# A decoder layer on one core: inverse at seven steps, first projections by operands as loaded, another order at the seam into the up projection

## The chip, the core and the metric

The kernel runs on one core of one Trainium2 chip. The core has TensorE (PE, the matrix engine; PEld is its loading of weights), VectorE (DVE), ScalarE (ACT), GpSimd (POOL) and SyncE (SP), which issues most of the DMAs. Every engine works through its own instructions in order and waits for others by semaphores. The metric is the device time of one execution in microseconds; less is better.

## The reference, cut

One layer of a hybrid decoder: 1024 tokens of width 1024, everything in float32.

```python
h = rms_norm(x, norm1_g);  proj = h @ w_in
p_rwkv, p_sb, q_mem, gate_logits = split(proj)
y_a = rwkv7_branch(p_rwkv, ...)             # 8 heads x 64: token shift, decay, delta-rule state over time
y_b = stick_breaking_branch(p_sb, ...)      # 8 heads x 64: causal, weights by cumulative log(1 - sigmoid)
y_m = memory_branch(q_mem, mem, ...)        # 4 heads x 128: softmax over 256 memory tokens
merged = sum_b sigmoid(gate_b) * (y_b @ w_branch[b])
x = x + merged @ w_out
h2 = rms_norm(x, norm2_g) @ w_up            # 1024 -> 5632
a = causal depthwise convolution of width 3 over h2, plus bias
x = x + (silu(a_gate) * a_val) @ w_down     # 2816 -> 1024
```

## The kernel before

**Arithmetic.** A product of float32 matrices is made of three matmuls on PE: each operand is split into a rounded part `hi` (a copy to fp32r, mostly on ACT) and a rest `lo` (operand minus `hi`, on POOL for weights, on DVE for activations), and hi x hi, hi x lo and lo x hi are added up in PSUM. A matmul takes a 128x128 block of one operand as weights and 512 columns of the other. Weight tiles are `wr` (as loaded), `wh` (L80) and `wl` (L81); `xhi` and `xlo` (L185, L186) are the split input.

**The order of the work.** Python writes the program; a scheduler in the tile framework then places each engine's instructions by priorities. Instructions that are `pinned` or kept in program order keep the order in which Python writes them; generators that `yield` are woven step by step (`weave`), so that a main chain of work and a stream of filler take turns.

1. `startup` (0 to 47 us): the parameters, three tiles of `w_in` (12, 13 and 4; 128x1024 each) and the eight row blocks of x are loaded by SP, one behind the other: weight, x, x, weight, and so on. All are split whole, ACT squares each block (L197), DVE adds the squares up as they come (L199), and for k in 0..7 PE multiplies block k with all three weights. The row norm goes in between at k = 4 and 6.
2. `rwkv_prep` (to some 300 us), woven with the filler `pump`: the rest of the projections, gates and the branches' first parts.
3. `sb_attn`, stick-breaking attention (300 to some 680 us), woven with `pump`. Its scans (L848) run on DVE; PE transposes what ACT makes of them (L860). Beside it the **inverse** of small triangular blocks runs on DVE: `inverse` has 62 steps of a product (L474, `it<-inst`) and a sum (L476, `inst<-inst,it`), and then 16 DMAs from the POOL queue (L483, `td<-inst`). `pumped` advances it by `pace[0]` / 10 of an instruction for each item of the filler; `pace[0]` is 6 from stick-breaking attention on. What is left is drained when the branches begin.
4. `mem_attn`, memory attention (680 to 775 us), in units of a head and half the tokens, woven with `pump`. A unit has a *front* (PE: `g<-A,qk`; DVE: maximum `mxt`, L1058, and its scaled negative `nb`, L1061; ACT: four exponentials, L1064; DVE: reciprocal and normalisation, L1068 and L1070), a *middle* (PE transposes; ACT copies them from `g` to `at`, L1079) and a *back* (PE: `mm<-at,A`; ACT copies the result, L1089). Round v has the front of unit v, the back of v-4 and the middle of v-2. The queries' own split is L1026 to L1028 (`qk`). The filler between them is a projection *gate*: ACT copies it out of PSUM (L749), DVE scales it by the row norm (L750, `w<-w,nrt`), ACT takes the sigmoid (L753). ACT loads another table between exponentials and the sigmoid.
5. `stage2` (the recurrence over time), group norm, branches, `out_proj` (775 to 1183 us). `out_proj` makes 128 tokens at a time (tt = 0..7): PE, then the residual sum and the squares (L1252 to L1254), the norm's power on POOL (L172, `ss<-rs,half`), and transposes into `raw0`, `raw1`.
6. **The seam** (1177 to 1222 us) and `up_phase` (to 1610 us). The up projection is a Strassen-Winograd product: per pair of weight columns 7 half-size products (numbers 1 to 7; 40 and 41 are the two parts of 4) in place of 8. Its operands on the token side are the blocks themselves ("11", "21", "22") and sums of them (T1 to T4), split by ACT and DVE or POOL (`hi`, `lo`; L1291, L1296). On the weight side POOL makes sums (L1402, L1403, L1414, L1415) and rests (L1386). `prep1`, `prep2` and `prep3` prepare a pair's weights; `step(n, i)` does product i of pair n and the sums on DVE (`u`: L1500, L1507, L1508, L1517, L1524; the memset of its first two columns L1438); `conv` is the convolution (L1446 to L1452). At the seam the last 128 tokens (columns 384 to 512 of the operands, `new`) are late, so pairs 0 and 1 run in an order of their own.
7. `down_phase` (1610 to 1824 us): 7 products x 11 steps. Each step splits an activation block `da` (L1654, L1656) and a weight block `dw` (L1655, L1657, or with a sum L1649) three steps ahead. `complete` adds a finished quarter of the output to the residual on DVE (L1676), `release` sends it out.

Of the kernel before, what the change touches and what calls it, by code (L numbers as in the profile page):

```python
# [19 lines left out]
D = 1024  # L20
C = 64
# [28 lines left out]
class Trunk:  # L50
# [70 lines left out]
    def setup(self):  # L121
# [11 lines left out]
        nc.sync.dma_start(self.params, self.I["params"])  # L133
# [34 lines left out]
    def rsqrt(self, out, ss, n, scale, eps):  # L168
        nc = self.nc
        t = self.small("rs", [128, 16])  # L170
        nc.vector.tensor_scalar(t[:, :n], ss, scale, eps, ALU.mult, ALU.add)
        nc.gpsimd.tensor_tensor(out, t[:, :n], self.half[:, :n], ALU.pow)  # L172

    def startup(self):
        nc = self.nc
        self.xhi, self.xlo, sqs, ws = [], [], [], []
        first = (12, 13, 4)
        for k in range(8):
            if k < 6 and k % 2 == 0:
                raww = self.load_w(self.I["w_in"][first[k // 2]])  # L180
            raw = self.t4("at")
            nc.sync.dma_start(raw, self.I["xT"][k * 128 : (k + 1) * 128, :])
            hi = self.pool_x.tile([128, 1024], F32R, name=f"xhi{k}")
            lo = self.pool_x.tile([128, 1024], F32R, name=f"xlo{k}")
            nc.scalar.activation(hi, raw, AF.Copy, scale=self.par("g1", k))  # L185
            nc.vector.scalar_tensor_tensor(lo, raw, self.par("g1", k), hi.bitcast(F32), ALU.mult, ALU.subtract)  # L186
            self.xhi.append(hi)
            self.xlo.append(lo)
            if k < 6 and k % 2 == 0:
                if k < 4:  # L190
                    hi = self.pool_wt.tile([128, 1024], F32R, name=self.nm("wh"), tag="wh", bufs=2)
                    lo = self.pool_wt.tile([128, 1024], F32R, name=self.nm("wl"), tag="wl", bufs=2)
                else:
                    hi, lo = self.t4(dt=F32R), self.t4(dt=F32R)
                ws.append(self.split_raw(raww, hi, lo))
            sq = self.t4("qk")
            nc.scalar.activation(sq, raw, AF.Square)  # L197
            if k:
                nc.vector.tensor_tensor(sq, sq, sqs[-1], ALU.add)  # L199
            sqs.append(sq)  # L200
        nc.sync.dma_start(self.kon, self.I["kon"])
        self.lora = self.t4("A")
# [3 lines left out]
        self.xin = lambda k: [[t[k][:, h * 512 : (h + 1) * 512] for h in range(2)] for t in (self.xhi, self.xlo)]  # L206
        pps = [[self.ps(t), self.ps(t)] for t in ("mm", "mm", "g")]
        for k in range(8):
            ks = slice(k * 128, (k + 1) * 128)
            for w, pp in zip(ws, pps):  # L210
                self.mm3(pp, [a[:, ks] for a in w], self.xin(k), k == 0, k == 7)
            if k == 4:
                self.row_norm(sqs[-1])
            elif k == 6:
                self.row_spread()
# [1001 lines left out]
    def out_proj(self):  # L1217
# [21 lines left out]
        def norm(tt, pp):  # L1239
            x = self.t4() if tt < 7 else l4("x7", F32)  # L1240
            sq = self.t4() if tt < 7 else self.pool_l.tile([128, 1024], F32, name="sq7", tag="sp", bufs=1)
            nc.sync.dma_start(x, self.I["x"][tt * 128 : (tt + 1) * 128, :])
            st = self.small("ss2", [128, 3])
# [8 lines left out]
            self.rsqrt(rs, rs, 1, 1.0 / D, 1e-6)  # L1252
# [54 lines left out]
        def late(tt):  # L1307
# [3 lines left out]
            elif tt == 5:  # L1311
                sums(0, 256)
            elif tt == 6:
                sums(256, 384)
# [13 lines left out]
        def weight_sums(w1):  # L1328
            w2, s = l4("wsec", F32), l4("wsum", F32)
            nc.sync.dma_start(w2, self.I["w_up"][1])  # L1330
            nc.gpsimd.tensor_tensor(s[:, :512], w2[:, :512], w2[:, 512:], ALU.add)
            nc.gpsimd.tensor_tensor(s[:, 512:], s[:, :512], w1[:, :512], ALU.subtract)
            self.early.append(self.split_raw(s, l4("wsh", F32R), l4("wsl", F32R)))
            nc.gpsimd.tensor_tensor(w2[:, :512], w1[:, :512], w2[:, :512], ALU.subtract)
            nc.gpsimd.tensor_tensor(s[:, 512:], w1[:, 512:], s[:, 512:], ALU.subtract)
# [7 lines left out]
        for tt in range(2, 8):  # L1343
            pp = mm((tt,), {3: (0,), 6: (1,)} if tt == 2 else {4: (tt - 1,)})[0]
            if tt == 5:
                weight_sums(w1)
# [571 lines left out]
```

## Time and profile before

| | |
|---|---|
| median of 3 runs | 1827.49 us (1827.4 to 1828.59) |
| profiled execution | 1825.74 us |
| its span | 1824.0 us |
| granted PE clock, mean | 0.995 |
| PE busy | 1785.2 us, 98% |
| DVE, ACT, POOL busy | 65%, 47%, 43% |
| first and last matmul | 7.79 and 1819.98 us |
| 90 matmuls of 512 columns at full speed | 20 us |

A row of the timeline gives start and length in us, engine, line, operation, `out<-in` by the names of the program, shapes, and in brackets how long the engine had been idle and what ended it. The waits list what PE waited for: total us, times, longest. PEclk is the granted share of the full TensorE clock.

### The profile page before, as it was taken

Reading aid. Unit: us, or ns where it says so; the run is one execution under the profiler, and the core shown is the slowest. Engines: PE = TensorE matmul, PEld = TensorE weight load, DVE = VectorE, ACT = ScalarE, POOL = GpSimd, SP = SyncE. Lnnn points to the kernel's source line nnn. Section 1 sums busy time; section 2 is a strip of 40 time slices with the busy share of each in tenths; the row PEclk is TensorE's granted clock in tenths of the full one; section 3 lists DMA queues with packets and bytes.
Section 4 is the critical chain, followed back from the end, with each engine's and each line's share of the span. In section 5 each row is a group of like instructions: output and inputs, shape, how many; then the busy total and the mean of one; then the engine's idle time right before and its main releaser. Section 6 shows DMA issues by size and latency. Waiting matters only on the chain.

```text
span 1824.0 us, 27302 instructions
## 1 busy us (share of the span) xinstructions
PE 1785.2 (98%) x10468; PEld 1444.6 (79%) x10468; DVE 1182.7 (65%) x1622; ACT 866.2 (47%) x1553; POOL 789.8 (43%) x447
## 2 busy tenths in 40 slices
PE   8999999999999999899999999989999999999999
PEld 6777778888787887677777878868888888888877
DVE  5667674787888854234542892487776777794595
ACT  5544344556566635434544333554544445444343
POOL 2323353322231433212323541587767777545454
PEclk9999999999999999899999999999999999999999
DMA  4255564211112323468754562322322323395475
GB/s 183 70 163 183 181 218 157 73 41 44 53 56 87 115 92 94 128 236 288 252 181 156 180 233 98 121 86 89 120 98 87 121 93 121 112 347 194 138 259 179
DMA packets 122341, 261.29 MB, mean 143 GB/s; under 512 B 28506, under 2 KB 43098, under 8 KB 122083
## 3 DMA queue, kind: packets, MB, share of 16 engines
q1 hardware_dynamic: 84738, 193.71, 32.3%
q10 hardware_dynamic: 33696, 53.23, 8.0%
q0 software_dynamic: 3776, 12.62, 2.3%
q8 instruction: 82, 1.34, 0.3%
q14 instruction: 49, 0.39, 0.1%
HBM read 178.99 MB, written 80.48 MB: 142 GB/s over the span
## 4 chain that ended last, share of the span: by engine, by line
PE 71%; DVE 3%; issue 3%; ACT 2%; POOL 2%; DMA 2%; SPq 0%; ACTq 0%; POOLq 0%; DVEq 0%
PE mm L115 58%; PE g L115 10%; PE g L105 3%; POOL dw L1657 1%; DVE at L1208 1%; DMA A<-yd 1%; DVE mg L1215 0%; DVE at L1207 0%; DVE w L750 0%; DVE inst L476 0%; DMA u<-in_w_down_dram 0%; DMA mrd<-w 0%; DMA x<-in_x_dram 0%; ACT w L753 0%; DMA wr<-in_w_out_dram 0%
## 5 line engine op out<-in xcount | busy, mean ns | idle before, releaser
L81 POOL TENSOR_TENSOR wl<-wr,wh 128x1024 fp32r<-128x1024 f32 x77 | 198.9, 2584 | 504.0 <-ACT wh L80 504.0
L115 PE MATMUL mm<-xhi,wh 128*128 128x512 f32 x784 | 262.2, 415 | 8.7 <-ACT xhi L185 7.8
L115 PE MATMUL mm<-xlo,wh 128*128 128x512 f32 x784 | 245.1, 394 | 0.9 <-DVE xlo L186 0.9
L115 PE MATMUL mm<-xhi,wl 128*128 128x512 f32 x784 | 243.1, 392 | 0.0
L115 PEld LDWEIGHTS mm<-xlo,wh 128*128 128x128 f32 x784 | 148.1, 189 | 34.7 <-DVE xlo L186 1.6
L115 PEld LDWEIGHTS mm<-xhi,wl 128*128 128x128 f32 x784 | 147.9, 189 | 33.3 <-POOL wl L81 0.5
L115 PEld LDWEIGHTS mm<-xhi,wh 128*128 128x128 f32 x784 | 137.8, 191 | 36.6 <-ACT xhi L185 7.8
L80 ACT ACTIVATE wh<-wr 128x1024 fp32r<-128x1024 f32 x77 | 81.6, 1060 | 145.7 <-PE mm L115 95.9
L115 PE MATMUL mm<-dw,da 128*128 128x512 f32 x528 | 121.2, 390 | 0.4 <-DVE da L1656 0.3
L115 PE MATMUL mm<-BT,l 128*128 128x512 f32 x504 | 117.9, 389 | 1.6 <-POOL l L1386 1.6
L1657 POOL TENSOR_TENSOR dw<-draw,dw 128x512 fp32r<-128x512 f32 x55 | 80.9, 1478 | 83.4 <-ACT dw L1655 83.4
L115 PEld LDWEIGHTS mm<-dw,da 128*128 128x128 f32 x528 | 98.9, 188 | 22.2 <-DVE da L1656 1.1
L848 DVE TENSOR_TENSOR_SCAN at<-at,nrt 128x128 f32<-128x128 f32 (+3 forms) x64 | 88.1, 1386 | 40.3 <-ACT at L842 40.2
L115 PEld LDWEIGHTS mm<-BT,l 128*128 128x128 f32 x504 | 94.5, 188 | 21.6 <-POOL l L1386 2.0
L115 PE MATMUL mm<-BT,wh 128*128 128x512 f32 x352 | 108.8, 390 | 1.6 <-DVE BT L1296 0.9
L115 PE MATMUL mm<-B,wh 128*128 128x512 f32 x352 | 108.5, 389 | 0.0
L1656 DVE TENSOR_TENSOR da<-draw,da 128x512 fp32r<-128x512 f32 x77 | 64.8, 851 | 59.6 <-ACT da L1654 57.1
L115 PE MATMUL g<-dw,da 128*128 128x512 f32 x396 | 92.5, 395 | 2.1 <-POOL dw L1657 1.1
L1386 POOL TENSOR_TENSOR l<-it,l 128x1024 fp32r<-128x1024 f32 x21 | 50.8, 2419 | 92.1 <-ACT l L1383 92.1
L115 PEld LDWEIGHTS g<-dw,da 128*128 128x128 f32 x396 | 75.4, 191 | 18.6 <-POOL dw L1657 1.4
L750 DVE TENSOR_TENSOR w<-w,nrt 128x1024 f32<-128x1024 f32 x24 | 48.8, 2033 | 63.6 <-ACT w L749 52.7
L1654 ACT ACTIVATE da<-draw 128x512 fp32r<-128x512 f32 x77 | 48.3, 629 | 81.5 <-PE mm L115 38.9
(332 smaller groups left out, 3987.1 us busy)
## 6 DMA issues: line engine op xcount, KB each, us to landing
wr<-in_w_in_dram SPq DMA_DIRECT2D x50, 512.0 KB, 3.6
draw<-actd SPq DMA_DIRECT2D x77, 256.0 KB, 3.4
draw<-in_w_down_dram SPq DMA_DIRECT2D x55, 256.0 KB, 4.6
at<-scr SPq DMA_DIRECT2D x24, 512.0 KB, 6.0
wr<-in_w_up_dram SPq DMA_DIRECT2D x22, 512.0 KB, 3.5
actd<-gall ACTq DMA_DIRECT2D x44, 256.0 KB, 3.2
rw<-in_w_up_dram SPq DMA_DIRECT2D x20, 512.0 KB, 3.6
gsd<-w ACTq DMA_DIRECT2D x18, 512.0 KB, 2.8
```

The lines of the kernel that those rows point to most:

```text
L80: self.nc.scalar.activation(hi, raw, AF.Copy)
L81: self.nc.gpsimd.tensor_tensor(lo, raw, hi.bitcast(F32), ALU.subtract)
L105: self.pinned(self.nc.tensor.transpose(out, in_, self.ident[:n, :n]))
L115: self.pinned(self.nc.tensor.matmul(*a, **k))
L750: nc.vector.tensor_tensor(g, g, self.nrb, ALU.mult)
L848: self.pinned(nc.vector.tensor_tensor_scan(sn[:, :W][:, ::-1], sn[:, :W][:, ::-1], self.nrt[:, 1152 - W :][:, ::-1], 1.0, ALU.mult, ALU.max))
L1208: nc.vector.tensor_tensor(g[:, hs], g[:, hs], o[:, hs], ALU.add)
L1386: nc.gpsimd.tensor_tensor(lo, src, hi.bitcast(F32), ALU.subtract)
L1654: self.pinned(nc.scalar.activation(A[:, 0], a, AF.Copy))
L1656: self.pinned(nc.vector.tensor_tensor(A[:, 1], a, A[:, 0].bitcast(F32), ALU.subtract))
L1657: nc.gpsimd.tensor_tensor(Wt[:, 1], w, Wt[:, 0].bitcast(F32), ALU.subtract)
```

## The change

The diff has four parts.

**Start.** The first weight tile comes in two parts of 256 and 768 columns; eight columns of the parameters come over the ACT queue first, the rest later. Eleven matmuls on a zeroed tile are put ahead of everything on PE. The first two blocks of x are split in halves, the products are written in the order in which their operands arrive, and the squares, their sums and the row norm come later.

```diff
-        nc.sync.dma_start(self.params, self.I["params"])
...
+        nc.scalar.dma_start(self.params[:, 0:8], self.I["params"][:, 0:8])
+        idle = self.t4("ys", BF16, 512)
+        nc.vector.memset(idle, 0.0)
+        pt = self.ps("g")
+        for _ in range(11):
+            nc.tensor.matmul(pt, idle[:, :128], idle, start=True, stop=True)
...
+            for hs in halves if k < 2 else [slice(0, 1024)]:
+                nc.scalar.activation(hi[:, hs], raws[k][:, hs], AF.Copy, scale=self.par("g1", k))
...
+        units(0, [0])
+        raw1 = self.load_w(self.I["w_in"][13])
+        load_x()
+        split_x()
+        ws.append(self.split_raw(raw1, *pair()))
+        units(0, [1])
...
+        units(1, [4])
+        self.row_norm(sqs[-1])
+        units(1, [5, 6, 7])
+        units(2, [4])
+        self.row_spread()
+        units(2, [5, 6, 7])
```

SP's queue at the start of the program, before (`wr`: weight tiles; `at`: blocks of x):

```order
L133 DMA params<-in_params_dram 128x246
L76 DMA wr_99<-in_w_in_dram 128x1024
L182 DMA at_101<-in_xT_dram 128x1024
L182 DMA at_113<-in_xT_dram 128x1024
L76 DMA wr_122<-in_w_in_dram 128x1024
L182 DMA at_124<-in_xT_dram 128x1024
L182 DMA at_137<-in_xT_dram 128x1024
L76 DMA wr_146<-in_w_in_dram 128x1024
```

and with the change (`it` is here the third weight tile):

```order
L224 DMA wr_119<-in_w_in_dram 128x256
L189 DMA at_121<-in_xT_dram 128x1024
L189 DMA at_127<-in_xT_dram 128x1024
L76 DMA wr_141<-in_w_in_dram 128x1024
L189 DMA at_143<-in_xT_dram 128x1024
L236 DMA wr_119<-in_w_in_dram 128x768
L189 DMA at_176<-in_xT_dram 128x1024
L245 DMA it_182<-in_w_in_dram 128x1024
```

The parameters have left the head of the queue, and the larger part of the first weight tile has moved behind the second weight tile and a third block of x.

**Inverse.** The pace is 7 in stick-breaking attention and 16 in memory attention:

```diff
-        pace[0] = 6
+        pace[0] = 7
         need("sb0")
         self.weave(self.sb_attn(qk, need), pump, 1.03, 0)
         need("kv")
+        pace[0] = 16
         self.weave(self.mem_attn(mq, need), pump, 1.6, 0)
```

No instruction is added or taken away, but the scheduler's order in memory attention is another. DVE there before, from the front of unit 6 to that of unit 7 (`mxt_6489`, `mxt_6502`: unit 6; `mxt_6565`, `mxt_6578`: unit 7; `w<-w,nrt`: a gate):

```order
L1058 TENSOR_REDUCE mxt_6489<-g_6482 128x2
L1058 TENSOR_REDUCE mxt_6502<-g_6495 128x2
L750 TENSOR_TENSOR w_1174_6551<-w_1174_6551,nrt 128x1024
L1061 SCALAR_TENSOR_TENSOR nb_6491<-mxt_6489,hf_6461 128x2
L1061 SCALAR_TENSOR_TENSOR nb_6504<-mxt_6502,hf_6461 128x2
L1058 TENSOR_REDUCE mxt_6565<-g_6558 128x2
L1068 RECIPROCAL rc_6508<-sm_6481 128x4
L1061 SCALAR_TENSOR_TENSOR nb_6567<-mxt_6565,hf_6461 128x2
L1070 TENSOR_SCALAR at_6480<-at_6480,rc_6508 128x256 x4
L1058 TENSOR_REDUCE mxt_6578<-g_6571 128x2
L1061 SCALAR_TENSOR_TENSOR nb_6580<-mxt_6578,hf_6461 128x2
```

and the same place with the change (lines are those of the changed kernel):

```order
L1129 TENSOR_REDUCE mxt_6515<-g_6508 128x2
L1129 TENSOR_REDUCE mxt_6528<-g_6521 128x2
L1132 SCALAR_TENSOR_TENSOR nb_6517<-mxt_6515,hf_6489 128x2
L1132 SCALAR_TENSOR_TENSOR nb_6530<-mxt_6528,hf_6489 128x2
L1139 RECIPROCAL rc_6534<-sm_6507 128x4
L1141 TENSOR_SCALAR at_6506<-at_6506,rc_6534 128x256 x4
L1129 TENSOR_REDUCE mxt_6589<-g_6582 128x2
L1129 TENSOR_REDUCE mxt_6602<-g_6595 128x2
L821 TENSOR_TENSOR w_1176_6576<-w_1176_6576,nrt 128x1024
L1132 SCALAR_TENSOR_TENSOR nb_6591<-mxt_6589,hf_6489 128x2
L1132 SCALAR_TENSOR_TENSOR nb_6604<-mxt_6602,hf_6489 128x2
```

The gate's product has moved from between unit 6's maxima and its `nb` to between unit 7's. On ACT, unit 6's exponentials and the copies of unit 4's transposes (L1079) stand, accordingly, ahead of the gate's copies. At the front of the query split, one of the two `qk` of L1028 has moved from behind a later unit's maxima to ahead of them.

**Seam.** The last tile's x is loaded ahead of the weights of the next pairs; the loads of pairs 1 and 2 (their tags `rw` and `wr` exchanged) and the first two weight sums of pair 1 stand at the start of `up_phase`; POOL's other work keeps the order in which it is written; pair 0 and 1 have product 7 in a bank of its own, and pair 1 another order.

```diff
         prep1(0)
         prep1(1)
+        load(1)
+        load(2)
+        weight_sum(1)
...
-        order = (6, 5, 40, 7, 41, 3) if n == 1 else (1, 5, 6, 2, 7, 4, 3)
+        order = (5, 6, 7, 40, 41, 3) if n == 1 else (1, 5, 6, 2, 7, 4, 3)
...
+    def apart(n):
+        Bk = bank()
+        product(n, 7, Bk, True, True)
+        v = st[n, "u2"] = u_tile()
+        seam(n, nc.vector.tensor_tensor(v[:, L2], Bk, st[n, "u1"][:, R2], ALU.add))
+        seam(n, nc.vector.tensor_tensor(v[:, R2], st[n, "C"], v[:, L2], ALU.add))
```

POOL from the last tile's norm on, before (`ss`: the norm's power; `B`: rests of operand "22"; `it`, `s`: weight sums; `l`, `wl`: rests of weights):

```order
L172 TENSOR_TENSOR ss_1638_10570<-rs_10578,half 128x1
L1296 TENSOR_TENSOR B_1_0_10547<-A_9857,B_0_0_10545 128x2x384
L1296 TENSOR_TENSOR B_1_1_10548<-A_9858,B_0_1_10546 128x2x384
L1386 TENSOR_TENSOR wl_10684<-wsec_10343,wh_10683 128x1024
L1296 TENSOR_TENSOR B_1_0_10547<-A_9857,B_0_0_10545 128x2x128
L1296 TENSOR_TENSOR B_1_1_10548<-A_9858,B_0_1_10546 128x2x128
L1402 TENSOR_TENSOR it_10726<-wr_10648 128x512
L1403 TENSOR_TENSOR it_10726<-it_10726,wr_10647 128x512
L1386 TENSOR_TENSOR l_1653_10710<-wsum_10344,l_1652_10709 128x512
L1414 TENSOR_TENSOR wr_10648<-wr_10647,wr_10648 128x512
L1415 TENSOR_TENSOR s_1670_10821<-wr_10647,it_10726 128x512
L1386 TENSOR_TENSOR l_1657_10730<-it_10726,l_1656_10729 128x1024
```

and with the change:

```order
L1486 TENSOR_TENSOR it_10595<-rw_10588 128x512
L1487 TENSOR_TENSOR it_10595<-it_10595,rw_10587 128x512
L171 TENSOR_TENSOR ss_1645_10603<-rs_10611,half 128x1
L1370 TENSOR_TENSOR B_1_0_10572<-A_9879,B_0_0_10570 128x2x384
L1370 TENSOR_TENSOR B_1_1_10573<-A_9880,B_0_1_10571 128x2x384
L1370 TENSOR_TENSOR B_1_0_10572<-A_9879,B_0_0_10570 128x2x128
L1370 TENSOR_TENSOR B_1_1_10573<-A_9880,B_0_1_10571 128x2x128
L1472 TENSOR_TENSOR wl_10727<-wsec_10365,wh_10726 128x1024
L1472 TENSOR_TENSOR l_1658_10739<-wsum_10381,l_1657_10738 128x512
L1472 TENSOR_TENSOR l_1662_10770<-it_10595,l_1661_10769 128x1024
L1494 TENSOR_TENSOR rw_10588<-rw_10587,rw_10588 128x512
L1495 TENSOR_TENSOR s_1663_10773<-rw_10587,it_10595 128x512
```

The two sums of pair 1 have moved ahead of the norm's power, the second rests of "22" ahead of pair 0's `wl`, and pair 1's `l<-it` two sums forward.

**Down.** `complete` becomes a generator that makes one sum per step, as does `last_residual`; finished tiles are sent out at steps 4 and 8 of a product rather than 3; a step's preparation is written ahead of the weights' sums.

```diff
+                        if y is terms[-1]:
+                            puts.append((half, n, tt, x[tt]))
+                        yield
...
             if f == 0:
-                complete()
-            elif f == 3:
+                rest = complete()
+            next(rest, None)
+            if f in (4, 8):
                 release()
```

257 lines of the change are left out of this document (169 added, 88 removed).

## The prediction

> **What bounds the kernel now.** I read the page first: is TensorE (PE) the limit, and where is it not?
>
> ```profile
> span 1824.0 us, 27302 instructions
> PE 1785.2 (98%) x10468; PEld 1444.6 (79%) x10468; DVE 1182.7 (65%) x1622; ACT 866.2 (47%) x1553; POOL 789.8 (43%) x447
> PEclk9999999999999999899999999999999999999999
> ```
>
> PE is busy for 1785.2 of 1824.0 us, so everything that can be won without taking matmuls away is the 38.8 us that it is idle, and the time that it runs at a lower granted clock (one slice of the page shows an 8). Next, who ends PE's idle time, from the waits of PE (line waited for: total, times, longest):
>
> ```profile
> PE g L115 <- ACT at L1079: 8.2, 1, 8.2
> PE mm L115 <- ACT xhi L185: 7.8, 1, 7.8
> PE mm L115 <- DVE qk L1028: 3.2, 1, 3.2
> PE g L105 <- ACT at L860: 2.3, 3, 1.1
> PE mm L115 <- DVE u L1508: 1.6, 1, 1.6
> PE mm L115 <- POOL l L1386: 1.6, 1, 1.6
> PE g L115 <- POOL dw L1657: 1.1, 1, 1.1
> PE g L115 <- ACT dw L1655: 1.0, 1, 1.0
> PE mm L115 <- DVE BT L1296: 0.9, 1, 0.9
> PE mm L115 <- DVE u L1438: 0.7, 1, 0.7
> PE g L105 <- ACT sq L1254: 0.7, 1, 0.7
> PE mm L115 <- ACT l L1383: 0.4, 1, 0.4
> ```
>
> Four places hold nearly all of it: the start (L185), memory attention (L1079, L1028), the seam into the up projection (L1508, L1386, L1296, L1438, L1254, L1383) and one hitch in the down projection (L1655, L1657). Last the stretches, to see the clock there (us, then busy time of PE, PEld, DVE, ACT, POOL, the granted PEclk, DMA share, GB/s):
>
> ```profile
> 0.00:20.00 20.00, 11.31 (x35) 8.64 (x36) 12.65 (x14) 15.75 (x16) 7.63 (x7) 1.00 0.91 352
> 300.00:620.00 320.00, 317.06 (x2191) 259.92 (x2191) 254.02 (x226) 195.23 (x356) 88.67 (x37) 1.00 0.19 60
> 720.00:740.00 20.00, 18.04 (x104) 13.29 (x104) 4.41 (x12) 4.86 (x11) 5.42 (x7) 0.91 0.32 80
> 740.00:760.00 20.00, 12.94 (x52) 10.48 (x53) 6.67 (x17) 11.40 (x26) 3.52 (x3) 0.74 0.38 110
> 1200.00:1220.00 20.00, 16.57 (x70) 12.40 (x68) 12.78 (x23) 10.64 (x14) 19.84 (x13) 1.00 0.19 56
> 1420.00:1440.00 20.00, 20.00 (x90) 16.57 (x89) 17.70 (x25) 10.00 (x14) 14.20 (x8) 1.00 0.34 120
> 1760.00:1780.00 20.00, 17.91 (x71) 14.10 (x70) 17.66 (x22) 7.71 (x14) 9.65 (x7) 0.91 0.72 246
> ```
>
> 1420:1440 is what full speed looks like: 90 matmuls of 512 columns in 20 us, 0.222 us each. Three stretches show a clock under 1.00, each just behind PE's waits: in memory attention and in the down projection a wait is paid for twice.
>
> **The change, part by part.**
>
> *Start.* The first weight tile arrives whole, is split on ACT, then the first row block of x is, and only then PE starts, at half speed:
>
> ```profile
> 5.27 1.06 ACT L80 ACTIVATE wh<-wr 128x1024 fp32r<-128x1024 f32 x1 [3.25 <-DMA wr<-in_w_in_dram]
> 7.79 1.22 PE L115 MATMUL mm<-xhi,wh 128*128 128x512 f32 x2 [7.79 <-ACT xhi L185]
> 14.34 1.05 PE L115 MATMUL mm<-xlo,wh 128*128 128x512 f32 x2
> 16.67 0.62 PE L115 MATMUL mm<-xlo,wh 128*128 128x512 f32 x2
> 46.47 0.61 PE L115 MATMUL g<-xhi,w 128*128 128x512 f32 x2
> ```
>
> The three projections (8 row blocks x 3 weights x 3 terms x 2 halves = 144 matmuls) run from 7.79 to 47.08, 39.3 us; at 0.222 us they need 32.0, and the two groups of small transposes in between add an estimated 2. So 7.8 us of waiting and some 5.3 us of slow clock and stutter can be won at most, 13.1. What stays: the first load has to come (landing ahead of 5.27), and the x blocks and weights, 5.5 MB, need 5.5 / 0.352 = 16 us at the rate of that stretch, so that the units ordered by arrival stay tied to DMA until about 17 us. The new order has a quarter of the weight tile and halves of x at the start: on ACT 1.06 / 4 + 1.06 / 2 = 0.8 in place of 2.1, 1.3 us less, and the parameters no longer stand ahead of the first load (some 0.4, estimated): real work from about 6.1. The 11 dummy matmuls need only a memset and should have the clock up by then. With 48 matmuls done by 17.6 us, the other 96 take 21.8 at 0.227 and the small ones 2: the end comes at about 41.5, against 47.1. That is -5.6; bounds -3 (x comes late, the clock is up no earlier) and -7.5 (both gains whole, and the wait for the row norm gone).
>
> *Inverse at seven steps.* The same 62 pairs of instructions run on DVE, only sooner:
>
> ```profile
> L474 DVE TENSOR_TENSOR it<-inst 128x62 f32<-128x62 f32 (+30 forms) x62 | 65.3, 1054 | 1.0
> L476 DVE TENSOR_TENSOR inst<-inst,it 128x62 f32<-128x62 f32 (+30 forms) x62 | 63.2, 1019 | 0.9
> 472.15 3.25 DVE L476 TENSOR_TENSOR inst<-inst,it 128x990 f32<-128x990 f32 x1
> ```
>
> They lie between 294 and 687 us: 128.5 us in 393, a third of DVE. At 7 in place of 6 they end near 294 + 393 x 6/7 = 631. In 300:620 that puts about 320 x (128.5/393) / 6 = 17.4 us more on DVE: 254.0 becomes 271.4 of 320, 85%. PE is idle for 2.9 us there now, mostly behind single long DVE instructions like the one at 472.15. Below zero it can hardly come (there is only 2.9 to win); above, if the waits grow as the busy share does against the idle (66 us left to 49), 2.9 x 66/49 = 3.9, +1.0; if a collision more or two of 3.25 us come through, +5. I take +1.5.
>
> *Memory attention.* The pace decides what DVE meets in its order. Before, the gate's product w<-w,nrt (L750) stands ahead of the two small nb of head unit 6, and waits for the gate's copies on ACT, which wait for PE:
>
> ```profile
> 738.48 1.06 ACT L80 ACTIVATE wh<-wr 128x1024 fp32r<-128x1024 f32 x1 [2.58 <-PE mm L115]
> 740.54 2.50 DVE L750 TENSOR_TENSOR w<-w,nrt 128x1024 f32<-128x1024 f32 x1 [7.65 <-ACT w L749]
> 742.96 0.22 DVE L1061 SCALAR_TENSOR_TENSOR nb<-mxt,hf 128x2 f32<-128x2 f32 x2
> 745.86 0.56 ACT L1064 ACTIVATE at<-g,nb,hf 128x256 f32<-128x256 f32 x1
> 747.06 2.93 PE L115 MATMUL g<-A,qk 128*128 128x256 f32 x12 [8.17 <-ACT at L1079]
> 714.61 1.69 PE L115 MATMUL g<-A,qk 128*128 128x256 f32 x12 [0.41 <-ACT at L1064]
> 762.30 1.04 PE L105 MATMUL g<-kon,at 128*128 128x128 f32 x8
> ```
>
> In the new order those nb come directly after their maxima, unit 6's exponentials and both copies of unit 4's transposes (L1079, they hold the banks `g` that PE wants) stand on ACT ahead of the gate's wh, and w<-w,nrt comes behind the maxima of unit 7. So PE's next 12 matmuls need not wait: -8.2. And the first half of the queries' qk (L1028) stands ahead of the next unit's maxima, not behind: -3.2. The clock: 0.91 and 0.74 over 20 us each are 1.8 + 5.2 = 7.0 us of missing pulses, part of them while PE waited anyway. The 12 matmuls took 2.93 against 1.69, +1.2; for the work behind both waits I take 2.4 more, about half of what is then left of the 7.0. Sum -15; bounds -11.4 (waits alone) and -17. What is late next: unit 6's transposes (762.30), which take the banks `g` of unit 7's front when its exponentials have read them. They would come about 11 us sooner, at 751.3. Unit 7's nb stand behind w<-w,nrt: that ends near 743, the sigmoid and a table load take 2.9 as from 742.96 to 745.86, then four exponentials and a copy of about 0.55 each: 748.7. That leaves 2.6 us of cover.
>
> By rows, the clock dropped after a 3.2 us wait (0.91) and in the down projection after two of 1.0 and 1.1 with matmuls between (0.91). The Trainium skill (TensorE: Matmul & The Clock Gate, Part 1) says that the clock halves after an idle window of about 3.4 us; by that page the small waits would cost no clock, and the down projection's term would be 2.1 rather than 3.9. The rows differ from it, and I go by the rows.
>
> *Seam.* POOL is full in 1200:1220 (19.84 of 20), and PE's waits there end on its results or on a DVE sum directly ahead of use:
>
> ```profile
> 1181.03 1.13 POOL L172 TENSOR_TENSOR ss<-rs,half 128x1 f32<-128x1 f32 x1 [5.80 <-DVE rs L171]
> 1197.49 1.61 POOL L1402 TENSOR_TENSOR it<-wr 128x512 f32<-128x512 f32 x1 [1.29 <-DMA wr<-in_w_up_dram]
> 1205.05 2.38 POOL L1386 TENSOR_TENSOR l<-it,l 128x1024 fp32r<-128x1024 f32 x1
> ```
>
> Two sums of pair 1 (1.61 + 2.16, as they run now at 1197.49) go into the idle 5.80 us ahead of 1181.03, with loads moved up for them: l<-it then comes some 3.8 us sooner, and the waits on L1386 (1.6) and L1383 (0.4) go. Product 40 between 7 and 3 covers the sum at L1508 (1.6), and the convolution's order the memset at L1438 (0.7). Of L1254 and L1296 (1.6) I count a sixth. Sum -4.5; bounds -6 and 0: ss now stands on POOL behind the sums, and they wait for two loads.
>
> *Down.* The adds of a finished half stood in one block on DVE and delayed the operands of the next steps; now one add goes with each step. -1.0 and -1.1, and the clock of 1760:1780, 20 x 0.09 = 1.8: -4 rounded; bounds -2 and -4.
>
> Sum: -5.6 + 1.5 - 15 - 4.5 - 4 = -27.6. The profiled execution took 1825.74 (its span 1824.0 and 1.74 around it), the median of the runs shown 1827.49, 1.75 more. 1827.5 - 27.6 = 1799.9: I say 1800.
>
> **The rivals.**
>
> *The stall in memory attention only moves* (chance 0.15). For it: w<-w,nrt still waits for ACT, which waits for PE, and unit 7's exponentials are behind it as unit 6's were. Against: the 2.6 us of cover, and past it each microsecond costs one, not eight. If half of the 15 comes back, 1807.5; if all but the first stall does, 1811.
>
> *POOL is late for the last tile's norm* (0.10). ss waits behind two sums that wait for two loads of 512 KB issued just before. For it: POOL runs strictly in order. Against: 5.80 us idle. If the loads land 4 us late, PE waits 4 more at L1254: the seam's gain is gone, 1804.5.
>
> *The start stays cold* (0.08): if the dummies end before x is split by more than a short wait, the clock falls again, and of 5.6 some 2.5 are left: 1803. The change would there not do what it says.
>
> *DVE becomes the limit of stick-breaking attention: slower* (0.03). The place is 300 to 631 us, 64 head units of about 5 us. The change adds about 17 inverse instructions to 300:620 (17.4 us at 1.04), and they push DVE's scans, which PE's transposes wait for (L860). To cancel the gains, PE would have to lose 27.6 us. If all 118 inverse instructions that would lie there (124 x 320/337) held a scan up by 0.3 us each, it would cost 35 us in place of the 1.5 counted: 1800 - 1.5 + 35 = 1833. It decides where a unit's DVE work is longer than PE's 5 us; now it is 254/64 = 4.0, then 4.2. So I find it unlikely. What speaks for it are rows like 472.15, three times the mean: POOL's split wl ran beside it.
>
> The Trainium skill (SBUF — State Buffer, section on the shared port pair) has a VectorE instruction with two inputs in SBUF blocked for as long as a GpSimd one runs; by that rule, the seam's earlier POOL sums and the denser inverse would both lengthen DVE's work beside them, which is a second road to this rival's end.
>
> **How the numbers follow.** My forecast, all four parts mostly as summed: 0.60, around 1800 (1793 to 1806 by the bounds). Rivals 0.15, 0.10, 0.08, 0.03; 0.04 is left for what I don't see: a quarter of it faster, half the same, a quarter slower. The range 1791 to 1812 reaches from the largest gains together (-7.5 - 17 - 6 - 4 = -34.5, 1793, and two of the 2.9 us in 300:620) to the first rival's far end. 0.2% (3.65 us) is about what a measurement here can tell. Faster by more: 0.94; same: 0.02; slower: 0.04.
>
> **What would show it.** Right: PE's waits have no row for L1079's or L1028's successors over 1 us; 740:760 shows a clock of 1.00; the first real matmul at about 6 us and the last of the three projections at 41 to 42; the inverse's last instruction near 631; PE over 19 in every 20 us of 1180:1240; 1760:1780 with 90 matmuls. Wrong: a wait of several us behind w<-w,nrt's users at unit 7; ss later than 1182; a PE idle time in 300:620 of over 6 us.

## The result, and the profile after

The change makes the kernel faster, by about half of what was forecast: 1813.24 us (median of 4 runs, 1811.42 to 1814.16) against 1827.45 (1826.69 to 1828.59); the ratio is 0.992, with a 95% interval of 0.9903 to 0.9938. The forecast was 1800, with a range to 1812. The profiled execution took 1813.44, its span 1811.7. First the page, and PE's waits with it:

```profile
span 1811.7 us, 27315 instructions
PE 1786.5 (99%) x10479; PEld 1444.0 (80%) x10479; DVE 1187.5 (66%) x1625; ACT 864.6 (48%) x1556; POOL 790.6 (44%) x448
```

```profile
PE g L105 <- ACT at L931: 4.0, 3, 3.0
PE g L105 <- ACT sq L1328: 3.3, 1, 3.3
PE mm L115 <- DVE u L1616: 2.8, 1, 2.8
PE mm L115 <- POOL wl L81: 1.7, 1, 1.7
PE mm L115 <- POOL l L1472: 1.4, 1, 1.4
PE g L182 <- DVE offs L159: 1.2, 1, 1.2
PE g L105 <- ACT w L1328: 1.2, 1, 1.2
```

(Lines have moved: L931 was L860 before, L1328, the norm's scaling ahead of the transposes, was L1254; L1616, the sum behind product 7, was L1508; L1472, the weights' rests, L1386.) The waits of 8.2 and 3.2 in memory attention and the two in the down projection are gone. Four rows are new or larger: L931 in stick-breaking attention, L81 behind the memory's weights, L1328 and L1616 in the seam. The stretches say the same (columns as in the prediction):

```profile
0.00:20.00 20.00, 18.55 (x68) 11.93 (x69) 10.86 (x17) 16.15 (x19) 8.14 (x8) 1.00 0.92 357
300.00:620.00 320.00, 315.43 (x2148) 258.01 (x2147) 266.38 (x240) 192.47 (x353) 85.40 (x36) 0.99 0.19 60
620.00:640.00 20.00, 18.32 (x163) 16.84 (x163) 7.08 (x11) 11.10 (x20) 12.20 (x7) 1.00 0.53 169
740.00:760.00 20.00, 20.00 (x90) 14.65 (x89) 3.85 (x6) 12.98 (x24) 2.38 (x1) 1.00 0.44 153
1160.00:1180.00 20.00, 16.73 (x73) 13.79 (x72) 15.48 (x31) 13.51 (x31) 10.34 (x6) 0.91 0.22 79
1220.00:1240.00 20.00, 16.93 (x66) 13.01 (x65) 17.12 (x22) 8.73 (x12) 19.68 (x12) 0.91 0.46 158
1760.00:1780.00 20.00, 20.00 (x90) 16.38 (x89) 18.22 (x19) 9.64 (x17) 11.84 (x9) 1.00 0.89 292
```

740:760 has 90 matmuls at full clock where there were 52 at 0.74, and 1760:1780 has 90 for 71. Two stretches of the seam stand at 0.91, which before had 1.00. To weigh the seam as a whole I take 1140 to 1260, which holds it in both kernels; before:

```profile
1140.00:1260.00 120.00, 114.18 (x513) 92.75 (x512) 78.33 (x134) 61.94 (x106) 84.44 (x52) 1.00 0.28 97
```

and after:

```profile
1140.00:1260.00 120.00, 110.43 (x478) 89.26 (x478) 86.22 (x136) 59.81 (x99) 82.29 (x50) 0.97 0.28 92
```

PE is idle for 9.6 us there, where it was 5.8, and the clock is lower besides. The seam, forecast at -4.5, has lost.

### The profile page after: what moved, and what is told of

Same layout as the page of the kernel before. It is cut to its first block, busy times and chain, and to the rows that moved or that the text cites. A ratio compares the mean times of both kernels' runs of the same rounds, so it can differ in the third digit from the quotient of the medians.

```text
span 1811.7 us, 27315 instructions
## 1 busy us (share of the span) xinstructions
PE 1786.5 (99%) x10479; PEld 1444.0 (80%) x10479; DVE 1187.5 (66%) x1625; ACT 864.6 (48%) x1556; POOL 790.6 (44%) x448
## 5 line engine op out<-in xcount | busy, mean ns | idle before, releaser
L81 POOL TENSOR_TENSOR wl<-wr,wh 128x1024 fp32r<-128x1024 f32 (+2 forms) x78 | 196.5, 2520 | 504.5 <-ACT wh L80 494.9
L80 ACT ACTIVATE wh<-wr 128x1024 fp32r<-128x1024 f32 (+2 forms) x78 | 81.8, 1048 | 146.3 <-PE mm L115 85.8
L1472 POOL TENSOR_TENSOR l<-it,l 128x1024 fp32r<-128x1024 f32 x21 | 51.7, 2460 | 90.1 <-ACT l L1471 90.1
L115 PEld LDWEIGHTS g<-dw,da 128*128 128x128 f32 x396 | 74.3, 188 | 15.6 <-POOL dw L1777 0.2
```

Of the source, the lines that this page charges most:

```text
L80: self.nc.scalar.activation(hi, raw, AF.Copy)
L81: self.nc.gpsimd.tensor_tensor(lo, raw, hi.bitcast(F32), ALU.subtract)
L115: self.pinned(self.nc.tensor.matmul(*a, **k))
L1472: fix(nc.gpsimd.tensor_tensor(lo, src, hi.bitcast(F32), ALU.subtract))
```

## The experiments

**Which part gives what.** Four kernels are the kernel before with the functions of one part taken from the changed one.

```diff
 start_alone:   setup, startup            from the changed kernel
 inverse_alone: run (pace 7 and 16)       from the changed kernel
 seam_alone:    rsqrt, out_proj, up_phase from the changed kernel
 down_alone:    down_phase                from the changed kernel
```

> The kernel before with the new start alone. Theory A (the parts are worth what their stretches of the trace say, and the seam is the one that lost): -4.6 us, about 1822.9, the same as the shift of the first matmul behind the three projections (47.58 to 42.95). Theory B (the loss in the changed kernel comes from parts acting on each other, and each alone gives what was forecast): -5.6, about 1821.9. Both: first real matmul near 5.8, no clock under full after 7 us.

> The kernel before with pace 7 and 16 alone. Theory A: the 15 to 16 us of memory attention are won, less about 3.6 in stick-breaking attention, 1.8 behind a weight split near 630 and 1 later: -10, about 1817. Theory B: -13.5 as forecast, about 1814.

> The kernel before with the changes of the out projection and the up phase alone. Theory A: the new order itself costs, by the norm's power behind two weight sums (+4.3 with the clock), the sums of gall ahead of product 7's (+4.5) and tile 6's norm (+1.3), less the waits removed (-5): +5 to +6, about 1833. Theory B: the order is good by itself and was hurt by what reaches it in the changed kernel: -4.5, about 1823.

> The kernel before with the new down projection alone. Both theories: the hitch near 1767 goes, with the halved clock behind it, and the small waits near 1619: -4 to -5, about 1823. If less comes, DMA is late there in its place.

Measured, against 1827.36 for the kernel before on the same chip: start 1822.16 (ratio 0.9972, interval 0.9961 to 0.9982), inverse 1815.83 (0.9941, 0.9922 to 0.996), seam 1831.52 (1.0024, 1.0014 to 1.0034), down 1820.77 (0.9966, 0.9952 to 0.998). So the seam's change alone makes the kernel slower, by 4.2 us, theory A. The other three are -5.2, -11.5 and -6.6; start and inverse lie between the two theories, and down gives more than either had. In the trace of `inverse_alone` a wait of 2.9 us for the last tile's norm stands in the seam of before, where the kernel before has 0.7: the load of x for that tile came late there (DVE idle for 2.70 us). It is not in the kernel of the next experiment (0.2), so it does not belong to the inverse wherever that runs.

**The three without the seam.** The changed kernel with `rsqrt`, `out_proj` and `up_phase` of before.

> The changed kernel with the out projection and the up phase of before: start, inverse and down projection alone. If the parts add up (-5.2, -11.5 and -6.5 as measured alone against 1827.4): about 1804, clearly under the changed kernel. If they act on each other: about 1813 or more.

1805.53 (0.9882, 0.9865 to 0.9899). The ratios of the three parts alone add up to -5.1 - 10.8 - 6.2 = -22.1, and this is -21.1 by the medians: nothing here shows them acting on each other. With the seam's change 1813.24 is reached: it costs 7 to 8 us in their company. PE in the same stretch, for this kernel:

```profile
1140.00:1260.00 120.00, 114.39 (x504) 92.86 (x503) 85.54 (x142) 60.39 (x98) 78.24 (x49) 0.99 0.29 97
```

It is idle for 5.6 us there, as before the change.

**Which pace.**

```diff
 pace_6_16:  pace[0] = 6 in stick-breaking attention, 16 in memory attention
 pace_7_7:   pace[0] = 7 in both
```

> The changed kernel with pace 6 in stick-breaking attention and 16 in memory attention. Theory A (the order of DVE in memory attention comes of how far the inverse is when it begins, so of the 7): the gate's product stands ahead of unit 6's nb as before, both stalls are back, +14 to +16, less 3 in stick-breaking attention: about 1825. Rival (the 16 brings the order): faster by 3, about 1810.

> The changed kernel with pace 7 throughout. Theory A (the 7 brings the gain): the order of the gate is the same, and the time within 1.5 us, 1812 to 1815. Rival: the stalls are back, about 1826.

1824.31 (0.9983, 0.9974 to 0.9993) and 1813.78 (0.9925, 0.991 to 0.9939). With 6 and 16, PE's waits have the old rows again:

```profile
PE g L115 <- ACT at L1150: 8.2, 1, 8.2
PE g L105 <- ACT sq L1328: 3.5, 1, 3.5
PE mm L115 <- DVE qk L1099: 3.4, 1, 3.4
```

8.2 and 3.4 as in the kernel before. The gain of memory attention comes from the 7 alone; the 16 does nothing that can be measured, since with 7 the inverse has ended at 627, before memory attention begins. With 6 and 16 it also ended ahead of it, at 660 (687 before the change), and the stalls are there all the same, with w<-w,nrt again between unit 6's maxima and its nb. So the pace matters through the order that the scheduler gives DVE, not by work being done sooner.

**The dummies.** The changed kernel without its eleven matmuls on zeros.

```diff
-        for _ in range(11):
-            nc.tensor.matmul(pt, idle[:, :128], idle, start=True, stop=True)
```

> The changed kernel without the eleven matmuls on zeros. Theory A (they raise the clock before the real work, and the order by arrival keeps PE fed): the first real matmuls show 1.05 us a pair until about 12 us, +2 to +3, about 1816. Rival (the clock would be up soon enough, PE waits for operands then anyway): within 1 us.

1812.80 (0.9922, 0.9906 to 0.9938): no difference. PE's timeline of this kernel:

```profile
5.94 1.41 PE L115 MATMUL mm<-xhi,wh 128*128 128x512 f32 x2 [5.94 <-ACT xhi L196]
8.00 1.05 PE L115 MATMUL mm<-xlo,wh 128*128 128x512 f32 x2
8.85 0.72 PE L115 MATMUL mm<-xhi,wh 128*128 128x512 f32 x2
```

and of the changed one:

```profile
1.19 4.82 PE L182 MATMUL g<-ys 128*128 128x512 bf16 x11 [1.19 <-DVE offs L159]
5.76 1.11 PE L115 MATMUL mm<-xhi,wh 128*128 128x512 f32 x2
8.26 0.61 PE L115 MATMUL mm<-xhi,wh 128*128 128x512 f32 x2
42.95 1.09 PE L115 MATMUL mm<-xhi,wh 128*128 128x512 f32 x2 [0.40 <-DVE w L322]
```

The dummies do raise the clock (a pair takes 0.6 from 6.71 on, and 1.05 until 8.85 without them), but the same pair of products starts at 8.26 against 8.85, and of these 0.6 us only 0.1 is left where the next projection begins, at 42.95 against 43.04. The start's gain is that of the order by arrival.

**One stall of the seam at a time.** The two that I held for the cause: POOL's power `ss` for the last tile is behind two weight sums, which wait for their loads; and DVE's four sums over `gall` stand ahead of the sum behind product 7.

```diff
 norm_first:
         load(2)
-        weight_sum(1)
...
         lo("22", old, eng=nc.gpsimd)
+        weight_sum(1)
         step(0, 1)
 act_sums_early:
-                if n == 2:
-                    act_sums(pairs[1][1], False)
...
-                if pairs[n][2] and n > 1:
+                if pairs[n][2]:
```

> The changed kernel with the two early weight sums of pair 1 put on POOL behind the last tile's power ss and the older rests of operand 22, not ahead of ss; the loads stay where they are. Theory A (ss was late because POOL waited for the loads in order): ss runs at about 1167.7 in place of 1170.7, PE's wait ahead of the last tile's transposes falls from 3.4 to about 0.5, and no halved clock follows: -4, about 1809. Rival (the tile was late for another reason, the residual sums or squares): no change.

> The changed kernel with the first two sums over gall of pair 1 written where the kernel before had them, at the end of pair 1, not at product 6 of pair 2. Theory A: DVE's block of four sums (7.4 us) ahead of the sum behind product 7 shrinks to two or less, PE's wait of 2.8 and the halved clock behind it go: -3 to -5, about 1809. Rival (DVE is full there anyway, and the sums stand in the way wherever they are): within 1 us.

1812.57 (0.9921, 0.9907 to 0.9936) and 1813.66 (0.9929, 0.9913 to 0.9946): neither moves the time. Yet the first edit does what it was meant for. POOL and PE in the changed kernel:

```profile
1167.50 1.29 POOL L1486 TENSOR_TENSOR it<-rw 128x512 f32<-128x512 f32 x1 [4.85 <-DMA rw<-in_w_up_dram]
1168.87 1.86 POOL L1487 TENSOR_TENSOR it<-it,rw 128x512 f32<-128x512 f32 x1
1170.69 1.26 POOL L171 TENSOR_TENSOR ss<-rs,half 128x1 f32<-128x1 f32 x1
1173.19 1.97 PE L105 MATMUL g<-kon,sq 128*128 128x128 f32 x8 [3.27 <-ACT sq L1328]
```

POOL stood for 4.85 us until the weights landed, with `ss` behind, and PE waited 3.27 for it. With `norm_first`, `ss` is early and the same eight transposes hardly wait; but PE waits now for a weight's rest, further on, 3.1 us at 1186:

```profile
1168.32 1.20 POOL L171 TENSOR_TENSOR ss<-rs,half 128x1 f32<-128x1 f32 x1 [5.14 <-DVE rs L170]
1170.75 1.09 PE L105 MATMUL g<-kon,sq 128*128 128x128 f32 x8 [0.28 <-ACT sq L1328]
1181.11 3.13 POOL L1370 TENSOR_TENSOR B<-A,B 128x256 fp32r<-128x256 f32 x2 [4.78 <-ACT B L1365]
1184.21 2.34 POOL L1472 TENSOR_TENSOR wl<-wsec,wh 128x1024 fp32r<-128x1024 f32 x1
```

```profile
PE mm L115 <- POOL wl L1472: 4.4, 2, 3.1
```

`wl<-wsec` stands behind two rests of operand "22" that POOL waits 4.78 us for: that is the move of the third POOL fence of the change, which the prediction passed over. In `act_sums_early`, PE's wait moves by one sum:

```profile
PE mm L115 <- DVE u L1606: 3.7, 1, 3.7
```

**Two at a time.**

```diff
 norm_wl (on top of norm_first):
         step(1, 2)
+        prep3(0)
...
         lo("22", new, eng=nc.gpsimd)
-        prep3(0)
 gall_late: all four sums over gall of pair 1 behind product 7's two sums
+                if n == 2:
+                    act_sums(pairs[1][1], False)
+                    act_sums(pairs[1][1], True)
```

> The changed kernel with the last tile's power ss ahead of pair 1's weight sums, as in the run before, and pair 0's rest wl<-wsec back ahead of the newest rests of operand 22 on POOL. Theory C (two stalls in a row hide each other: with ss early, PE only waits later, for wl<-wsec, 3.3 us and a halved clock behind it, since POOL sat idle for 5 us ahead of the rests that stand before it): now both go, -4 to -6, about 1808. Rival (POOL as a whole is the limit of the seam, and a third wait takes the time): within 1 us of 1813.

> The changed kernel with all four sums over gall of pair 1 put behind product 7's two sums on DVE. Theory C (the four sums need to be made before pair 2's convolution only, and hold up nothing there but what stands behind them): PE's wait of 2.8 goes and its halved clock, -4, about 1809. Rival (DVE is the limit between pairs 1 and 2, whatever the order): the wait shows up behind the difference of product 4 or at the next pair's first sum, and the time is within 1 us of 1813.

1812.25 (0.992, 0.9905 to 0.9935) and 1815.63 (0.9935, 0.992 to 0.995). In `norm_wl` the wait for the rest is 1.8 (POOL's subtraction took 4.03 us there, for 2.34 in `norm_first`), the one for pair 2's rest l<-it is 1.7, and the 2.8 for the sum behind product 7 is as before; in `gall_late` the wait for u is replaced by a larger one:

```profile
PE mm L115 <- POOL wl L1472: 4.3, 1, 4.3
```

**POOL's order for pair 2, and everything at once.**

```diff
 sum2_first:
-                if n > 1:
+                if n > 2:
                     weight_sum(n)
...
                 if n == 1 and i == 6:
+                    weight_sum(nxt)
                     prep1(nxt)
 mended = norm_first + sum2_first + prep3(0) directly behind step(0, 2) + tile 6's norm ahead of sums(0, 256, (1,))
 mended_gall = mended + gall_late
```

> The changed kernel with the first two weight sums of pair 2 put on POOL ahead of pair 2's rest wl<-wr, not behind it. Theory D (POOL's idle 6.2 us at 1199.5, where wl<-wr waits for ACT in order, push everything on POOL behind it into the gall sums, and both slow each other): the sums fill the idle time, the wait for l<-it (1.4) goes, POOL is ahead by 2.6 us in 1220 to 1240: -2 to -4, about 1810. Rival (POOL was waiting for work, and its lateness there costs nothing): within 1 us of 1813.

> The changed kernel with the last tile's power ahead of the weight sums, pair 0's rest wl<-wsec directly behind product 2 of pair 0, pair 2's sums ahead of its rest, and tile 6's norm ahead of the block sums. Theory C (stalls in a row hide each other, all must go): -7 to -9, about 1805. Rival (POOL and DVE are full in the seam): within 2 us of 1812.

> As the run before, with the four sums over gall behind product 7's sums as well. Theory C: the wait of 2.8 and its clock go too, 3 to 4 under the run before, about 1802. Rival: as in the run where this was done alone, PE waits for POOL's next rest in its place, no gain.

1811.49 (0.9923, 0.9908 to 0.9938), 1811.25 (0.9921, 0.9906 to 0.9936) and 1812.69 (0.9927, 0.9912 to 0.9941): theory C falls as well (in `mended_gall` PE waits 3.4 us for DVE in pair 2 and 2.1 in pair 3). The waits of `mended` in the seam:

```profile
PE mm L115 <- DVE BT L1370: 2.8, 1, 2.8
PE mm L115 <- DVE u L1615: 2.4, 1, 2.4
PE mm L115 <- DVE u L1605: 2.3, 1, 2.3
```

and its stretch:

```profile
1140.00:1260.00 120.00, 111.15 (x483) 90.17 (x482) 87.23 (x137) 59.51 (x99) 82.49 (x50) 0.97 0.28 94
```

8.9 us idle. Neither POOL (82 of 120 us) nor DVE (87) is full over this stretch: each stands in order behind something of the other or of ACT. In 1220:1240 POOL was full in the changed kernel (19.68 of 20); in `mended` it has 15.6 there, and the time is the same.

**ACT ahead of the convolution.** In these kernels DVE idles for 5 us before pair 1's convolution, because ACT stands waiting for a POOL result ahead of it; then it has all of it at once.

```diff
 conv_first (on top of sum2_first): pair 1's convolution on ACT, and pair 2's last weight split, in the order written
-            nc.scalar.activation(c, u[:, ...], AF.Identity, ...)
+            (ordered if n == 1 else lambda ins: ins)(nc.scalar.activation(c, u[:, ...], AF.Identity, ...))
-            w = hl(w2, self.pool_wt, ("wh", "wl"), keep=n < 2)
+            w = hl(w2, self.pool_wt, ("wh", "wl"), keep=n < 3)
 conv_norm = conv_first + norm_wl + tile 6's norm first
```

> The changed kernel with pair 2's first weight sums ahead of its rest (as in the run where only this was done) and pair 1's convolution on ACT kept ahead of pair 2's last weight split. Theory E (DVE was idle for 5 us because ACT stood waiting for POOL ahead of the convolution, and then had all of it at once): ACT's convolution of pair 1 starts 4 to 5 us sooner, DVE's first sum of pair 2 is in time, PE's waits for u (3.8 with the clock behind them) go: -3 to -5 against 1811.5, about 1807.5. Rival (the sums over gall and the convolution are too much for DVE there at any order): within 1 us of 1811.5.

> As the run before, with the last tile's power ahead of pair 1's weight sums, pair 0's rest wl<-wsec ahead of the newest rests of operand 22, and tile 6's norm ahead of the block sums. Theory E and C: the stalls at the seam's start go as well, 3 us under the run before, about 1804, as good as the seam of before with pair 1's new order (1803.8). Rival: a wait of 2 to 3 us for a DVE or POOL rest stays at the seam's start, about 1807.

1813.74 (0.9925, 0.9912 to 0.9937) and 1811.27 (0.9918, 0.9904 to 0.9932). The convolution on ACT in the changed kernel, then in `conv_first`:

```profile
1211.74 2.17 ACT L1545 ACTIVATE g<-u,params 128x512 f32<-128x512 f32 x3
```

```profile
1207.80 2.19 ACT L1545 ACTIVATE g<-u,params 128x512 f32<-128x512 f32 x3 [1.41 <-DVE u L1625]
```

It comes 3.9 us sooner, and PE's waits for u are gone but for one of 0.25, as theory E said. But the time stays, since the rests of the weights are late in their place:

```profile
PE mm L115 <- POOL wl L1472: 5.0, 3, 3.0
```

**One piece of the seam by itself.** The kernel without the seam's changes, with pair 1's order of products alone.

```diff
-            order = (6, 5, 40, 7, 41, 3) if n == 1 else (1, 5, 6, 2, 7, 4, 3)
+            order = (5, 6, 7, 40, 41, 3) if n == 1 else (1, 5, 6, 2, 7, 4, 3)
...
+                elif n == 1 and i == 7:
+                    apart(n)
...
-                if i == (6 if n > 1 else 5):
+                if i == 6:
                     prep2(nxt)
```

> The changed kernel with the seam of before, and of the seam's changes only pair 1's order: product 7 into a bank of its own, then 4, then 3. If this piece does what was argued (product 4 covers the sum ahead of product 3): the waits of 1.6 and 0.7 on u go, -2 to -2.5 against the kernel with the seam of before, about 1803. If a POOL rest is late instead: within 1 us of 1805.5.

1803.79 (0.9883, 0.9867 to 0.99), the lowest median here, 1.7 under 1805.53; but the kernels before beside which the two were timed differ by 0.9 (1825.69 and 1826.61), and the ratios are the same (0.9883, 0.9882), so a gain in time is not shown. In the trace the piece does what was argued; its stretch:

```profile
1140.00:1260.00 120.00, 116.36 (x515) 95.17 (x514) 88.82 (x146) 60.39 (x97) 80.97 (x51) 0.99 0.29 97
```

3.6 us idle for 5.6; no wait for u is left among its waits.

## Why the prediction was wrong, point by point

**The seam is the step that failed.** It was summed at -4.5 with bounds -6 and 0; it measured +4.2 alone and +7 to +8 in company. That is 12 us of the 13 that the forecast was off. Matched matmuls show where. The first column below goes from the out projection's products for the last tile (`mm<-qk,mg`) to pair 1's products 5 and 6 (`mm<-BT,l`), the second from there to pair 2's product 1 (`mm<-B,wh`), the third from there to pair 3's products 5 and 6 (`mm<-BT,l`), in us of each kernel's trace:

| | last tile and pair 0 | pair 1 | pair 2 |
|---|---|---|---|
| before | 39.95 | 18.34 | 21.76 |
| seam's change alone | 42.07 | 13.60 | 28.82 |
| changed kernel | 44.86 | 13.60 | 28.84 |
| changed kernel, seam of before | 39.53 | 20.21 | 21.76 |

What was summed came true: in pair 1 the waits of 1.6, 1.6 and 0.7 are gone, and it is 4.7 us shorter. What the sum put at nothing is the rest of the path: pair 2, which ran without a wait before, takes 7.1 us longer, and the last tile and pair 0 take 2.1 longer alone and 4.9 in company. The waits stand one pair further on, for pair 2's l<-it and for its sum behind product 7; in the changed kernel:

```profile
1214.34 5.28 PE L115 MATMUL mm<-BT,l 128*128 128x512 f32 x22 [1.39 <-POOL l L1472]
1231.26 4.60 PE L115 MATMUL mm<-B,l 128*128 128x512 f32 x12 [2.79 <-DVE u L1616]
```

and the second of them with the seam's change alone:

```profile
1243.08 3.02 PE L115 MATMUL mm<-B,l 128*128 128x512 f32 x12 [2.79 <-DVE u L1545]
```

The step took away the waits that it named in pair 1; what it did not do is to follow what every moved instruction is then put behind. At the last tile, the idle 5.80 us on POOL that the two sums were to fill was gone when they could start: the loads had landed at 1167.50, DVE's part of the norm was done at 1167.70, and `ss` came at 1170.69, behind the sums. The second rival ("POOL is late for the last tile's norm") did happen so, with 3.3 us for the 4 given, but it had a chance of 0.10 and was taken to cost only what the seam had won. And it was not alone: `wl<-wsec` behind the rests of "22", which stood in the order, was costed at nothing; pair 2's rest ahead of its sums held POOL for 6.2 us; the sums over `gall` came in a block of four, a move that the prediction did not name. The bound of 0 allowed for no loss at all, and of a part that moves work on three engines that run in order, a loss can't be excluded. The range was narrower than the bounds of its own parts besides: -3, +5, -11.4, 0 and -2 add up to -11.4, which is 1816 and not 1806.

Part of the difference between +4.2 and +7 to +8 is the clock. Alone, the seam's stretches of 20 us all have 1.00; in the changed kernel two of them have 0.91, 1.8 us each, and without the seam's change one.

Taking stalls away, one or several, gave nothing that can be measured: the ratios of the nine kernels tried lie between 0.9918 and 0.9935, within the interval of the changed kernel (0.992, 0.9903 to 0.9938). In all nine traces pair 1 keeps its gain (3.8 to 4.8 us) and pair 2 its loss (5.2 to 8.5). Why the seam stays there in every order tried but the one of before is not settled by one cause: shown is that in each trace another instruction of POOL, ACT or DVE is late by 2 to 4 us, that none of the three is full over the 120 us, and that removing one brings out the next. That the loads at the seam's start, or the orders kept by force on all three engines, are the root was not tried apart. Tile 6's norm (1.2 at L1328) was not mended by putting it ahead of the sums either (1.0 in `mended`). Of the prediction's own signs, the one for the seam failed: PE was to have over 19 in every 20 us of 1180:1240, and has 19.3, 18.6 and 16.9.

**Memory attention** was right. The same matmul, matched in both traces, starts 1.2 us later than before at 634 (633.79 for 632.59), and 15.4 us earlier at 757 (757.21 for 772.59): 16.6 us won between, for the 15 forecast. The stalls went whole, the clock with them, and the cover at unit 7 held. Its first rival did not occur.

**The inverse** went the way that was argued and costs more: +1.5 was taken, with +5 as the bound; matched matmuls are 4.3 us ahead of before at 373 (373.09 for 377.40) and only 0.75 at 591 (590.66 for 591.41): 3.6 lost between, the clock included (0.84 in 470:480). DVE is busy for 266.4 of 320 (271.4 was worked out), and the one long wait is that chain which the prediction knew from memory attention, in the changed kernel:

```profile
469.25 2.35 POOL L81 TENSOR_TENSOR wl<-wr,wh 128x1024 fp32r<-128x1024 f32 x1
469.31 3.38 DVE L882 SCALAR_TENSOR_TENSOR qk<-w,params,qk 64x1024 fp32r<-64x1024 f32 x1
472.72 1.18 DVE L547 TENSOR_TENSOR inst<-inst,it 128x980 f32<-128x980 f32 x1
473.81 1.22 DVE L821 TENSOR_TENSOR w<-w,nrt 128x1024 f32<-128x1024 f32 x1
475.06 1.06 ACT L824 ACTIVATE w<-w 128x1024 f32<-128x1024 f32 x1 [5.38 <-DVE w L821]
476.66 0.96 PE L105 MATMUL g<-kon,at 128*128 128x128 f32 x4 [2.99 <-ACT at L931]
```

A gate's sigmoid stands on ACT ahead of the copy that PE needs, and waits for DVE, which is behind a long product and an inverse step. One more loss was not foreseen, 1.7 us at 630 (L81): the inverse's DMAs now share POOL's queue with the splits of the memory's weights, one `td<-inst` directly ahead of the late one. POOL stood idle for 3.02 us with that DMA next in its order, until the inverse's last sum was done, while ACT's half of the weight had been ready since 623.9. Together that is somewhat past the bound of +5; pace 7 and 16 alone are -11.5, where -13.5 was forecast. The inverse ended at 627 (631).

**The start**: -5.2 alone, -4.6 by the trace, for -5.6; the first matmul at 5.76 (6.1), the end of the three projections at 42.1 (41.5). Right, though not for the dummies' sake.

**Down**: -6.6 alone for -4 by the medians, though the interval (-3.7 to -8.8) takes in its bound of -4, and the profiled executions are 4.9 apart; beside the hitch at 1767 small waits near 1619 and 1720 (0.3 and 0.1) are gone as well.

## What to carry to other kernels

A wait that is taken away is worth its length only if the next result that the waiting engine needs is not late too; in a stretch where three engines feed a fourth, each in order and with 50 to 75% of the time, look at what stands ahead of each operand in the new order, down to the second and third and past the end of the part that was reordered, before counting the sum of the waits as a gain. Time such a stretch by itself, against the one before: here three parts of the change were worth 22 us, and the fourth, which had been made to remove some 6 us of waits, took a third of that back. A change of pace can be worth more by the order that a scheduler makes of it than by the work that it moves.

## What the runs showed of the hardware that was not expected

PE's clock fell behind waits that are shorter than the Trainium skill (TensorE: Matmul & The Clock Gate, Part 1: The HAM clock gate) has for it: 0.91 in 1220:1240 behind a wait of 2.8, and 0.91 in 1760:1780 before the change behind two of 1.0 and 1.1 with a matmul between, where the page speaks of an idle window of about 3.4 us. The length of one wait does not decide it, though: behind the 2.79 us for the same sum, the 12 matmuls took 4.60 in the changed kernel and 3.02 with the seam's change alone (3.01 in `norm_first`, behind 2.78), and the 1.7 us at 630 left the clock at 1.00. What does decide it was not tried. At the start a pair of matmuls was down to 0.72 us 2.9 us after the first matmul without dummies (5.94 to 8.85), somewhat sooner than that page's 3.4 us of sustained work for the way up.

Beside POOL's work, DVE's sums of two tiles in SBUF took far longer. In the kernel before, two of the sums over `gall` ran while POOL idled (1229.99 to 1233.00), 0.71 each:

```profile
1230.94 1.42 DVE L1463 TENSOR_TENSOR gall<-gall 128x512 f32<-128x512 f32 x2
1233.00 2.83 POOL L1386 TENSOR_TENSOR l<-it,l 128x1024 fp32r<-128x1024 f32 x1 [3.01 <-ACT l L1383]
```

The other two, from 1232.89 on, beside that subtraction, took 1.74 each. In the changed kernel the four came while POOL ran without a gap, 1.85 each:

```profile
1222.48 7.38 DVE L1569 TENSOR_TENSOR gall<-gall 128x512 f32<-128x512 f32 x4
```

The Trainium skill (SBUF — State Buffer, Who interferes with whom) has a VectorE sum of two SBUF operands and a GpSimd instruction that reads SBUF contend for a shared port pair, whichever comes first holding up the other; the trace agrees that both take longer (POOL's l<-it,l took 2.82 beside the four sums, 2.37 ahead of them). Against sums beside an idle POOL, 4 x (1.85 - 0.71) = 4.6 us is what it cost DVE in this block, 2.5 of it more than in the kernel before. The 4.6 is more than the 2.8 us that PE waited for the sum behind it, but moving the block (`gall_late`) did not win the time, as above.
